# A hybrid mLSTM layer on one core: z and v projected with the tokens stationary, q moved ahead of z, PSUM banks divided three to five

## The chip, the cores and the metric

The kernel runs on 1 core of one Trainium2 chip. The metric is the device time of one execution in microseconds (us); lower is better. The kernel before takes 1349.28 us (median of 3 runs, 1349.18 to 1349.31). Engines are named as in the profile: PE (TensorE: matmuls; PEld are its weight loads), DVE (VectorE), ACT (ScalarE), POOL (GpSimd), SP (SyncE, which here issues the large loads).

## The reference

One layer on 256 prompt tokens and 64 sample tokens, width 2048, in float32:

```python
h = rmsnorm(x)
q, k, v, o, gates, u, z = split(h @ w_in)      # 512, 512, 1024, 1024, 8, 1024, 1024 columns
hm, C, n, m = mlstm_chunkwise(q, k / sqrt(128), v, ig, log_sigmoid(f), C0, n0, m0)  # 4 heads
y_m = rmsnorm_per_head(hm) * sigmoid(o)
zs = rmsnorm(gelu(z), g_sgu)                   # over the 1024 columns of z, per token
y_s = gelu(u) * (tril(w_sp) @ zs + b_sp)       # over chunks of 128 tokens
x = x + concat(y_m, y_s) @ w_out
x = x + square(relu(rmsnorm(x) @ w_ff1)) @ w_ff2
y = rmsnorm(x, g_final)
```

Outputs are y for both streams, the states C, n, m, and zs of the sample tokens. The token norm of the first line is put behind the projections: every projection is multiplied by R1, one factor per token.

## The kernel before

All 320 tokens (three blocks `TOK` of 128, 128 and 64) are worked on at once. Float32 precision is made of two reduced-precision parts: a weight tile is loaded (`raw`), ACT casts it to `hi`, DVE makes `lo = raw - hi`; activations are kept as `Xh`, `Xl` likewise. A product is hi·xh + hi·xl + lo·xh.

Most of the work stands in a list of jobs, run in order. A `Job` (L73) projects 128 output columns: the weight is stationary, 320 tokens move, 48 matmuls add up in one PSUM bank, and the result has columns on partitions and tokens along the row. `evac` then takes it out of the bank. The list begins with 8 jobs of z, 4 of q, 8 of v, 8 of o, 8 of u; then 16 of w_out and, four times, 16 of w_ff1 and 4 `Group`s of w_ff2 (L103). A `Group` has the tokens stationary instead: 512 weight columns move in 8 chunks of 2x128 rows, and the result comes out with tokens on partitions. k and the gates are projected in a loop of their own ahead of the list (`kacc`, `gacc`).

z and v are wanted with tokens on partitions (v as the moving operand of the heads, z for the spatial gating). So each of their jobs is followed by three transposes on PE into a bank (`zt`, `vt`), which DVE and ACT then read (`z_side`, `v_side`). The norm over z's columns is summed on POOL into `sacc`, and PE adds it up over the partitions (`ssz`).

Engines run their queues in the order of the code (a manual schedule). Smaller work is written as coroutines: `later(gen, d)` enters one, and `run_side`, called ahead of each job, runs the next piece of every coroutine that is due (`cur` counts the jobs). Such are the gate chain (`gates`), z's transposes, and the four heads. `head(h)` has three pieces:

- the scores S = k·q and the transposed k (`kt`) into two banks; DVE and ACT make P (`Pm`, `Ph`, `Pl`), `kh`, `kl` and others of them;
- 24 matmuls into three banks T and two more, `cs` and `cs2`; then DVE and ACT form the head's norm from T (`den`, `hsq`, `rsqrt_to`, `hmt`), and the new state `co` from `cs` and `cs2` (L611: `co` from `cs2`);
- six transposes of `hmt` (`hT`).

`v_evac` enters `head(i // 2)` after every second v job, so heads start two jobs apart. PSUM has 8 banks of 128x512 float32: 2 with the tag "mm" (`mmt`, for projections) and 6 with "sd" (`sdt`, everything else). A tile that wants a bank waits until what was in the bank has been read.

Weight halves are split (`split_until`) four ahead of the one that PE works on; ACT's and DVE's queues hold these splits between the evacuations and the pieces of the coroutines.

Of the kernel before, what the change touches and what calls it, by code (L numbers as in the profile page):

```python
# [50 lines left out]
def emit(tc, A):  # L51
# [51 lines left out]
    class Group:  # L103
# [6 lines left out]
        def __init__(self, src, q, g):  # L110
            self.src, self.q, self.g = src, q, g
            self.raw, self.hi, self.lo = ([None] * GC for _ in range(3))

        def load(self, c):
            self.raw[c] = wp.tile([P, 2, GN], F32, tag="raw", name=f"raw_g{self.q}{self.g}_{c}", bufs=4)
            sp.dma_start(self.raw[c][:], self.src[:, 2 * c:2 * c + 2, :])

        def split(self, c):
            hi = wp.tile([P, 2, GN], F32R, tag="hi", name=f"hi_g{self.q}{self.g}_{c}")
            lo = wp.tile([P, 2, GN], F32R, tag="lo", name=f"lo_g{self.q}{self.g}_{c}")  # L120
            act.copy(hi[:], self.raw[c][:])  # L121
            dve.tensor_tensor(lo[:], self.raw[c][:], hi.bitcast(F32)[:], ALU.subtract)  # L122
            self.hi[c], self.lo[c] = hi, lo

        def matmuls(self, after):

            n = f"{self.q}{self.g}"
            last = GC - 1
            back = sdt(f"gt{n}") if self.q == QUARTERS - 1 else None
            ga = [mmt(f"ga{n}_0"), mmt(f"ga{n}_1"), sdt(f"ga{n}_2")]  # L130
            gl = [sdt(f"gl{n}_{m}") for m in range(GM)]
            for c in range(GC):
                for kk in range(2):
                    k = 2 * c + kk
                    hi = self.hi[c][:, kk, :]
                    if k == 0:
                        pe.matmul(ga[2][:], hs[k][:], hi, start=True, stop=False)
                    for j in range(2):
                        t0, w = TOK[j]
                        pe.matmul(ga[j][:], hid[k][0][:, t0:t0 + w], hi, start=k == 0, stop=False)  # L140
                        pe.matmul(ga[j][:], hid[k][1][:, t0:t0 + w], hi, start=False, stop=k == KT - 1)  # L141
                    if k:
                        pe.matmul(ga[2][:], hs[k][:], hi, start=False, stop=k == KT - 1)  # L143
# [12 lines left out]
                after(c, back)  # L156
# [74 lines left out]
    for k in range(KT):  # L231
# [6 lines left out]
        act.activation(Xh[k][:], xr, AF.Copy, scale=gk)  # L238
# [8 lines left out]
        dve.scalar_tensor_tensor(Xl[k][:], xr, gk, Xh[k].bitcast(F32)[:], ALU.mult, ALU.subtract)  # L247
# [14 lines left out]
        for h in range(H):  # L262
            pe.matmul(kacc[h][:, :NT], hi[:, h * P:h * P + P], Xh[k][:], start=first, stop=False)
        for h in range(H):
            pe.matmul(kacc[h][:, :NT], hi[:, h * P:h * P + P], Xl[k][:], start=False, stop=False)
        for h in range(H):
            pe.matmul(kacc[h][:, :NT], lo[:, h * P:h * P + P], Xh[k][:], start=False, stop=last)
        pe.matmul(gacc[:100, :NT], hi[:, 4 * P:], Xh[k][:], start=first, stop=False)
        pe.matmul(gacc[:100, :NT], hi[:, 4 * P:], Xl[k][:], start=False, stop=last)
# [20 lines left out]
    zs = [None] * 4  # L290
    vT = [None] * 8
# [23 lines left out]
    rz = ap.tile([P, 3], F32, name="rz")  # L315
    Y = [None] * KT
# [31 lines left out]
    def gates():  # L348
# [5 lines left out]
        rsqrt_to(R1[:], s[:, :NT], D, tmp320, "r1")  # L354
        yield
# [83 lines left out]
    def z_evac(c):  # L439
        def evac(acc):  # L440
            t = tmp320(f"zr{c}")
            dve.tensor_tensor(t, acc, R1[:], ALU.mult)
            gz = tmp320(f"gz{c}")
            act.activation(gz, t, AF.Gelu_apprx_tanh)
            if c == 0:
                act.activation(sacc[:], gz, AF.Square)
                pool.tensor_scalar(sacc[:], sacc[:], D // 2 * EPS / P, None, ALU.add)
            else:
                act.activation(t, gz, AF.Square)
                pool.tensor_tensor(sacc[:], sacc[:], t, ALU.add)  # L450
            later(z_side(c, gz), 3 - c % 2)
        return evac

    def z_side(c, gz):
        if c == 0:
            z01 = ap.tile([P, 2, 8, P], F32, tag="big", name="z01", bufs=2)
            z2g = ap.tile([P, 2, 8, P], F32, tag="big", name="z2g", bufs=2)
            zs[:] = [z01[:, 0], z01[:, 1], z2g[:, 0], z2g[:, 1]]
            zs.append(z01)
            pool.memset(zs[2][NS:], 0.0)  # L460
            sp.dma_start(zs[3], A["gsgu"].partition_broadcast(P))
        pt = sdt(f"zt{c}")
        for j, (t0, n) in enumerate(TOK):
            pe.transpose(pt[:n, P * j:P * j + P], gz[:, t0:t0 + n], ident[:])
        dve.tensor_copy(zs[4][:, :, c, :], pt[:, 0:256].rearrange("p (j c) -> p j c", c=P))
        dve.tensor_copy(zs[2][:NS, c, :], pt[:NS, 256:384])
        if c < 7:
            return
        yield
        st = sdt("ssz")  # L470
        for j, (t0, n) in enumerate(TOK):
            pe.matmul(st[:n, 2 * j:2 * j + 2], sacc[:, t0:t0 + n], ones[:, 0:2], start=True, stop=True)
        s3 = small(P, 3)("z3s")
        pool.memset(s3, 1.0)
        for j, (t0, n) in enumerate(TOK):
            dve.tensor_copy(s3[:n, j:j + 1], st[:n, 2 * j:2 * j + 1])
# [35 lines left out]
    def v_evac(i):  # L512
        def evac(acc):
            t = tmp320(f"vT{i}")
            dve.tensor_tensor(t, acc, R1[:], ALU.mult)
            later(v_side(i, t), 2)
            if i % 2:
                later(head(i // 2), 2)
        return evac

    def v_side(i, t):
        h, e = divmod(i, 2)
        pt = sdt(f"vt{i}")
        for j, (t0, n) in enumerate(TOK):
            pe.transpose(pt[:n, P * j:P * j + P], t[:, t0:t0 + n], ident[:])
        vh, vl = vau_h[h % 2], vau_l[h % 2]
        for sl, n, c0, c1 in ((slice(0, 2), P, 0, 256), (slice(2, 3), NS, 256, 384)):
            src = pt[:n, c0:c1].rearrange("p (j c) -> p j c", c=P)
            dst = (slice(0, n), sl, slice(e * P, e * P + P))
            act.copy(vh[dst], src)  # L530
            dve.tensor_tensor(vl[dst], src, vh.bitcast(F32)[dst], ALU.subtract)
        return
        yield
# [140 lines left out]
    x2rhs = lambda k: (X2[k][0][:], X2[k][1][:])  # L674
# [24 lines left out]
    def out_evac(m):  # L699
        def evac(acc):  # L700
            dve.tensor_tensor(xres[m], acc, xres[m], ALU.add)
            h_ = xp.tile([P, NT], F32R, tag=f"xh{m}", name=f"x2h{m}")
            l_ = xp.tile([P, NT], F32R, tag=f"xl{m}", name=f"x2l{m}")
            act.activation(h_[:], xres[m], AF.Copy, scale=g2(m))
            dve.scalar_tensor_tensor(l_[:], xres[m], g2(m), h_.bitcast(F32)[:],
# [87 lines left out]
    halves = [(j, i) for j in jobs + [group] for i in range(GC if isinstance(j, Group) else 2)]  # L793
# [23 lines left out]
    for i, job in enumerate(jobs):  # L817
        cur[0] = i
# [6 lines left out]
        if i in pre:  # L825
            pre[i]()
        if isinstance(job, Group):
            def after(c, pt):
# [4 lines left out]
                if pt is not None and job.g == 0 and c == 3:  # L833
                    for i in range(8):
                        gfb.append(xp.tile([P, NT], F32, tag=f"xh{i}", name=f"gfb{i}"))
# [18 lines left out]
    ga = [mmt("ga0"), mmt("ga1"), sdt("ga2")]  # L854
# [109 lines left out]

def _arrays(i):
# [5 lines left out]
    for n, width in (("q", 512), ("k", 512), ("v", 1024), ("o", 1024), ("g", 8), ("u", 1024),  # L971
# [21 lines left out]
        "w_q": _tiles(cols["q"]), "w_v": _tiles(cols["v"]), "w_o": _tiles(cols["o"]),  # L993
        "w_u": _tiles(cols["u"]), "w_z": _tiles(cols["z"]),
# [33 lines left out]
```

## Time and profile before

| | |
|---|---|
| time, median of 3 runs | 1349.28 us |
| the profiled execution | 1349.38 us, span 1347.7 us |
| PE busy | 1337.1 us (99%) |
| DVE, ACT, POOL busy | 711.9, 563.7, 19.2 us |
| z jobs (with q) on PE | from 38.6 us |
| v jobs on PE | from 127.1 us |
| w_out jobs on PE | from 323.8 us |
| read from HBM | 202.7 MB |

A row of the timeline has its start, its length, engine, line, operation, output and inputs, and how many were merged (xN); in brackets, the idle time before it and what ended that. Matmuls overlap: their lengths add up to more than the time they take, so starts are compared.

### The profile page before, as it was taken

What the parts mean: (1) busy time and instruction counts of PE and PEld (TensorE: products, weight loads), DVE (VectorE), ACT (ScalarE), POOL (GpSimd) and SP (SyncE); (2) the same over time, 40 slices, a digit from 0 to 9 for tenths busy, and PEclk for the clock granted to TensorE, in tenths of its full rate; (3) what the DMA queues carried; (4) which work ended last, traced back from release to release, by engine and by line L of the source; (5) the groups of instructions that cost most, each with busy time, mean ns of one, the idle gap of its engine ahead of it and who ended that gap; (6) DMA issues with size and microseconds to landing.
All of it is one profiled execution on the core that took longest, in us unless ns stands there. A gap on an engine that the chain in (4) does not pass through costs nothing.

```text
span 1347.7 us, 20742 instructions
## 1 busy us (share of the span) xinstructions
PE 1337.1 (99%) x8409; PEld 1277.4 (95%) x8409; DVE 711.9 (53%) x1064; ACT 563.7 (42%) x907; POOL 19.2 (1%) x57
## 2 busy tenths in 40 slices
PE   9999999999999999999999999999999999999997
PEld 9999999999999999988999988899998889998885
DVE  8676565555555544444444454454444454444665
ACT  7544556444443444333344343234442334443333
POOL 1120000000000000000000000000000000000000
PEclk9999999999999999999999999999999999999999
DMA  8645433545444444445444355444445545445442
GB/s 277 212 147 184 130 131 113 171 140 195 166 157 154 138 147 157 157 141 159 150 145 156 126 169 163 152 141 157 152 145 159 155 127 170 149 145 185 132 141 78
DMA packets 60883, 208.01 MB, mean 154 GB/s; under 512 B 6816, under 2 KB 8736, under 8 KB 60788
## 3 DMA queue, kind: packets, MB, share of 16 engines
q1 hardware_dynamic: 57796, 200.53, 46.5%
q10 hardware_dynamic: 2960, 6.12, 1.3%
q8 instruction: 66, 1.08, 0.3%
q14 instruction: 29, 0.24, 0.1%
q0 software_dynamic: 32, 0.03, 0.0%
HBM read 202.72 MB, written 3.94 MB: 153 GB/s over the span
## 4 chain that ended last, share of the span: by engine, by line
PE 99%; DMA 0%; DVE 0%; ACT 0%; SPq 0%; issue 0%; DVEq 0%; ACTq 0%
PE acc_f L97 11%; PE acc_f L101 11%; PE acc_f L98 11%; PE gl L150 10%; PE ga L141 8%; PE ga L140 8%; PE ga L143 4%; PE acc_out L97 3%; PE acc_out L101 3%; PE acc_out L98 3%; PE acc_u L97 1%; PE acc_v L101 1%; PE acc_z L101 1%; PE acc_v L97 1%; PE acc_o L101 1%; PE acc_o L97 1%
## 5 line engine op out<-in xcount | busy, mean ns | idle before, releaser
L97 PE MATMUL acc_f<-x2h,hi_f 128*128 128x320 f32 x1024 | 302.6, 309 | 0.0
L98 PE MATMUL acc_f<-x2l,hi_f 128*128 128x320 f32 x1024 | 302.4, 309 | 0.0
L122 DVE TENSOR_TENSOR lo_g<-raw_g,hi_g 128x1024 fp32r<-128x1024 f32 x128 | 153.5, 1223 | 129.6 <-PE gl L150 88.1
L121 ACT CAST hi_g<-raw_g 128x1024 fp32r<-128x1024 f32 x128 | 132.2, 1049 | 200.4 <-PE ga L143 175.9
L97 PEld LDWEIGHTS acc_f<-x2h,hi_f 128*128 128x128 f32 x1024 | 192.3, 188 | 0.1
L98 PEld LDWEIGHTS acc_f<-x2l,hi_f 128*128 128x128 f32 x1024 | 192.2, 188 | 0.1
L140 PE MATMUL ga<-hi_g,Yh 128*128 128x512 f32 x480 | 188.7, 393 | 0.0
L141 PE MATMUL ga<-hi_g,Yl 128*128 128x512 f32 x480 | 188.4, 392 | 0.0
L87 DVE TENSOR_TENSOR lo_f<-raw_f,hi_f 128x1024 fp32r<-128x1024 f32 x128 | 151.5, 1222 | 59.4 <-ACT hi_f L86 39.3
L101 PE MATMUL acc_f<-x2h,lo_f 128*128 128x320 f32 x1024 | 171.0, 309 | 0.0
L150 PE MATMUL gl<-Yh,lo_g 128*128 128x320 f32 x960 | 159.7, 308 | 0.0
L150 PEld LDWEIGHTS gl<-Yh,lo_g 128*128 128x128 f32 x960 | 150.1, 188 | 9.5
L101 PEld LDWEIGHTS acc_f<-x2h,lo_f 128*128 128x128 f32 x1024 | 155.4, 188 | 0.0
L86 ACT CAST hi_f<-raw_f 128x1024 fp32r<-128x1024 f32 x128 | 128.8, 1046 | 37.5 <-PE ga L143 31.3
L729 ACT ACTIVATE f<-f 128x320 f32<-128x320 f32 x64 | 30.2, 472 | 254.3 <-DVE f L728 254.3
L140 PEld LDWEIGHTS ga<-hi_g,Yh 128*128 128x128 f32 x480 | 90.2, 188 | 16.4 <-DVE f L728 1.3
L141 PEld LDWEIGHTS ga<-hi_g,Yl 128*128 128x128 f32 x480 | 90.2, 188 | 16.0
L728 DVE SCALAR_TENSOR_TENSOR f<-acc_f,R 128x320 f32<-128x320 f32 x64 | 31.5, 492 | 132.5 <-PE acc_f L101 132.3
L143 PE MATMUL ga<-hi_g,hs 128*128 128x512 f32 x225 | 87.9, 391 | 0.0
L98 PE MATMUL acc_out<-Yl,hi_out 128*128 128x320 f32 x256 | 75.6, 309 | 0.0
L97 PE MATMUL acc_out<-Yh,hi_out 128*128 128x320 f32 x256 | 75.6, 309 | 0.0
L338 DVE TENSOR_TENSOR Yl<-f,Yh 128x320 fp32r<-128x320 f32 x64 | 31.5, 492 | 65.9 <-ACT Yh L337 65.9
(358 smaller groups left out, 1931.3 us busy)
## 6 DMA issues: line engine op xcount, KB each, us to landing
raw_f<-w_ff SPq DMA_DIRECT2D x128, 512.0 KB, 4.3
raw_g<-w_ff SPq DMA_DIRECT2D x128, 512.0 KB, 3.9
raw_out<-w_out SPq DMA_DIRECT2D x32, 512.0 KB, 4.6
raw_z<-w_z SPq DMA_DIRECT2D x16, 512.0 KB, 5.3
raw_v<-w_v SPq DMA_DIRECT2D x16, 512.0 KB, 5.2
raw_o<-w_o SPq DMA_DIRECT2D x16, 512.0 KB, 5.0
raw_u<-w_u SPq DMA_DIRECT2D x16, 512.0 KB, 4.6
w0raw<-w SPq DMA_DIRECT2D x15, 306.0 KB, 4.4
```

Source lines behind the costliest of these rows:

```text
L86: act.copy(hi[:], raw[:])
L87: dve.tensor_tensor(lo[:], raw[:], hi.bitcast(F32)[:], ALU.subtract)
L97: pe.matmul(o, self.hi[h][:, k, :], xh, start=(h == 0 and k == 0), stop=False)
L98: pe.matmul(o, self.hi[h][:, k, :], xl, start=False, stop=False)
L101: pe.matmul(o, self.lo[h][:, k, :], xh, start=False, stop=(h == 1 and k == 7))
L121: act.copy(hi[:], self.raw[c][:])
L122: dve.tensor_tensor(lo[:], self.raw[c][:], hi.bitcast(F32)[:], ALU.subtract)
L140: pe.matmul(ga[j][:], hid[k][0][:, t0:t0 + w], hi, start=k == 0, stop=False)
L141: pe.matmul(ga[j][:], hid[k][1][:, t0:t0 + w], hi, start=False, stop=k == KT - 1)
L143: pe.matmul(ga[2][:], hs[k][:], hi, start=False, stop=k == KT - 1)
L150: pe.matmul(gl[m][:, :NT], self.lo[c][:, kk, m * P:m * P + P], hid[k][0][:], start=k == 0, stop=k == KT - 1)
L338: dve.tensor_tensor(l_[:], src, h_.bitcast(F32)[:], ALU.subtract)
```

## The change

- z and v are no longer 16 `Job`s but 4 of a new kind, `Rows` (two groups of 512 columns each): tokens stationary, 512 weight columns moving, in 8 chunks of 16 matmuls. The three token blocks come out with tokens on partitions in three banks. For the third block, Xh and Xl of the 64 sample tokens are put side by side as one stationary operand of 128 columns (`pair`), whose two halves of the result are added.
- Xh and Xl become the halves of one tile.
- The transposes `zt` and `vt`, and the sums `ssz` on PE, are gone. R1 is also wanted by rows: it goes through DRAM (`rd`) into `rt`, with four DMAs on POOL's queue. ACT applies it while it applies gelu to z or casts v, and sums the squares of z.
- q's four jobs stand ahead of z; `q_evac` also makes the `pair` tiles, eight copies in each.
- Inside a `Rows` group, `cur` goes up ahead of chunks 2, 4 and 6, so a group has four steps of the coroutines.
- `v_evac` enters two heads at the end of a group, the first with a delay of 1 and the second of 2.
- Tag "mm" gets three banks and "sd" five; the third accumulator of a w_ff2 `Group` moves from "sd" to "mm".

```diff
-        return ps.tile([P, 512], F32, tag="mm", name=name, bufs=2)
+        return ps.tile([P, 512], F32, tag="mm", name=name, bufs=3)
...
-        return ps.tile([P, 512], F32, tag="sd", name=name, bufs=6)
+        return ps.tile([P, 512], F32, tag="sd", name=name, bufs=5)
...
+    class Rows(Chunks):
+        def __init__(self, src, name, evac):
+            super().__init__(src, name)
+            self.evac = evac
+
+        def matmuls(self, before, after):
+            acc = [mmt(f"ga_{self.name}_{j}") for j in range(3)]
+            for c in range(GC):
+                before(c)
+                for j, (t0, n) in enumerate(TOK):
+                    for k in (2 * c, 2 * c + 1):
+                        hi, lo = self.hi[c][:, k % 2, :], self.lo[c][:, k % 2, :]
+                        first, last = k == 0, k == KT - 1
+                        xh, xl = Xh[k][:, t0:t0 + n], Xl[k][:, t0:t0 + n]
+                        if j < 2:
+                            pe.matmul(acc[j][:], xh, hi, start=first, stop=False)
+                            pe.matmul(acc[j][:], xl, hi, start=False, stop=False)
+                            pe.matmul(acc[j][:], xh, lo, start=False, stop=last)
+                            continue
+                        if not first:
+                            pe.matmul(acc[j][:NS, :], xh, lo, start=False, stop=False)
+                        pe.matmul(acc[j][:], pair[k], hi, start=first, stop=last)
+                        if first:
+                            pe.matmul(acc[j][:NS, :], xh, lo, start=False, stop=False)
+                    if c == GC - 1:
+                        self.evac(j, acc[j])
+                after(c, None)
...
-            ga = [mmt(f"ga{n}_0"), mmt(f"ga{n}_1"), sdt(f"ga{n}_2")]
+            ga = [mmt(f"ga{n}_{j}") for j in range(3)]
...
+        rd = dr.tile([1, NT], F32, name="rd")
+        pool.dma_start(rd[:], R1[0:1, :])
+        for j, (t0, n) in enumerate(TOK):
+            pool.dma_start(rt[:n, j:j + 1], rd[0, t0:t0 + n].unsqueeze(1))
...
+    def z_evac(g):
+        def evac(j, acc):
...
+            z = zs[j][:n, 4 * g:4 * g + 4, :].rearrange("p a b -> p (a b)")
+            src = acc[:n, :]
+            if j == 2:
+                dve.tensor_copy(z, acc[:NS, :])
+                dve.tensor_tensor(z, acc[NS:, :], z, ALU.add)
+                src = z
+            act.activation(z, src, AF.Gelu_apprx_tanh, scale=rt[:n, j:j + 1])
+            for i in range(2):
+                t = tmp320(f"zq{g}{j}{i}")
+                act.activation(t[:n, :256], z[:, 256 * i:256 * i + 256], AF.Square,
+                               accum_out=zsq[:n, j, 2 * g + i:2 * g + i + 1])
+            if g and j == 2:
+                later(z_norm(), 1)
...
     def q_evac(h):
         def evac(acc):
             dve.tensor_tensor(qT[h][:], acc, R1[:], ALU.mult)
+            for k in range(4 * h, 4 * h + 4):
...
+                act.copy(pair[k][:, :NS], Xh[k].bitcast(F32)[:, NP:])
+                act.copy(pair[k][:, NS:], Xl[k].bitcast(F32)[:, NP:])
...
-            later(v_side(i, t), 2)
-            if i % 2:
-                later(head(i // 2), 2)
+    def v_evac(g):
+        def evac(j, acc):
+            n = TOK[j][1]
+            src = acc[:n, :]
+            if j == 2:
+                low = ap.tile([P, 512], F32, tag="gb", name=f"vs{g}", bufs=2)
+                dve.tensor_copy(low[:NS, :], acc[:NS, :])
+                dve.tensor_tensor(low[:NS, :], acc[NS:, :], low[:NS, :], ALU.add)
+                src = low[:NS, :]
+            r = rt[:n, j:j + 1]
+            for i in range(2):
+                vh, vl, x = vau_h[i], vau_l[i], src[:, DV * i:DV * i + DV]
+                act.activation(vh[:n, j, :DV], x, AF.Copy, scale=r)
+                dve.scalar_tensor_tensor(vl[:n, j, :DV], x, r, vh.bitcast(F32)[:n, j, :DV],
+                                         ALU.mult, ALU.subtract)
+            if j == 2:
+                later(head(2 * g), 1)
+                later(head(2 * g + 1), 2)
...
-    for c in range(8):
-        add(A["w_z"][c], z_evac(c), xrhs, f"z{c}")
     for h in range(H):
         add(A["w_q"][h], q_evac(h), xrhs, f"q{h}")
-    for i in range(8):
-        add(A["w_v"][i], v_evac(i), xrhs, f"v{i}")
+    for g in range(2):
+        jobs.append(Rows(A["w_z"][g], f"z{g}", z_evac(g)))
+    for g in range(2):
+        jobs.append(Rows(A["w_v"][g], f"v{g}", v_evac(g)))
...
+        if isinstance(job, Rows):
+            def before(c):
+                if c and c % 2 == 0:
+                    cur[0] += 1
+                    run_side()
+
+            def after(c, pt):
+                base[0] += 1
+                split_until(base[0] + 4)
+
+            job.matmuls(before, after)
+            continue
```

Where the heads stand moves with it. On PE before, head 1's scores and transposes stand here (S1 and kt1 are tiles of head 1, hT0 of head 0, vt3 and acc_v5 of v's jobs; the bracket names the engine whose work the instruction waits for):

```order
L618 MATMUL hT0_0_2068<-ident_144,hmt_615 128x128 [waits DVE_49,Activation_49]
L618 MATMUL hT0_0_2068<-ident_144,hmt_615 128x128 [waits Activation_49] x2
L618 MATMUL hT0_1_2074<-ident_144,hmt_615 128x128 x3
L525 MATMUL vt3_2080<-ident_144,vT3_1934 128x128 x2
L525 MATMUL vt3_2080<-ident_144,vT3_1934 64x128
L540 MATMUL S1_2088<-qT1_582,kT1_586 128x256
L541 MATMUL S1_2088<-qT1_582,kT1_586 128x128
L542 MATMUL S1_2088<-qT1_582,kT1_586 64x64
L545 MATMUL kt1_2092<-ident_144,kT1_586 128x128 [waits Activation_49]
```

On PE in the changed kernel they stand right behind the last matmuls of head 0's second piece (cs2 of head 0 is printed as cs20), ahead of chunk 2 of group v1:

```order
L611 MATMUL cs20_1774<-vauh0_581,kh_597 128x258
L612 MATMUL cs20_1774<-vaul0_583,kh_597 128x258
L613 MATMUL cs20_1774<-vauh0_581,kl_598 128x258
L577 MATMUL S1_1810<-qT1_566,kT1_570 128x256 [waits DVE_49]
L578 MATMUL S1_1810<-qT1_566,kT1_570 128x128
L579 MATMUL S1_1810<-qT1_566,kT1_570 64x64
L582 MATMUL kt1_1814<-ident_128,kT1_570 128x128 [waits Activation_49]
L582 MATMUL kt1_1814<-ident_128,kT1_570 128x128
L582 MATMUL kt1_1814<-ident_128,kT1_570 64x128
L138 MATMUL ga_v1_0_1702<-hi_v1_2_1628,x4_90 128x512
```

So S1 moved from behind hT0, with a v job between, to directly behind cs20, and it got a wait for DVE, kt1 one for ACT. Heads 2 and 3 stand to each other in the same way, behind job o0.

On DVE before, head 0's P stands behind the evacuation of one v job and the two halves of its transposed copy (`vaul0` from vt1):

```order
L87 TENSOR_TENSOR lo_v4_0_1821<-raw_v4_0_1672,hi_v4_0_1820 128x1024
L87 TENSOR_TENSOR lo_v4_1_1827<-raw_v4_1_1740,hi_v4_1_1826 128x1024
L515 TENSOR_TENSOR vT2_1830<-acc_v2_1769,R1_80 128x320
L531 TENSOR_TENSOR vaul0_599<-vt1_1832,vauh0_597 128x2x128
L531 TENSOR_TENSOR vaul0_599<-vt1_1832,vauh0_597 64x128
L548 TENSOR_TENSOR P0_1848<-S0_1840,Ea0_1538 128x256
```

On DVE in the changed kernel it stands behind the evacuation of the whole group v0 and a split:

```order
L565 SCALAR_TENSOR_TENSOR vaul0_583<-ga_v0_0_1455,rt_609,vauh0_581 128x256
L565 SCALAR_TENSOR_TENSOR vaul1_584<-ga_v0_0_1455,rt_609,vauh1_582 128x256
L565 SCALAR_TENSOR_TENSOR vaul0_583<-ga_v0_1_1456,rt_609,vauh0_581 128x256
L565 SCALAR_TENSOR_TENSOR vaul1_584<-ga_v0_1_1456,rt_609,vauh1_582 128x256
L558 COPY vs0_1656<-ga_v0_2_1457 64x512
L559 TENSOR_TENSOR vs0_1656<-ga_v0_2_1457,vs0_1656 64x512
L565 SCALAR_TENSOR_TENSOR vaul0_583<-vs0_1656,rt_609,vauh0_581 64x256
L565 SCALAR_TENSOR_TENSOR vaul1_584<-vs0_1656,rt_609,vauh1_582 64x256
L118 TENSOR_TENSOR lo_v1_3_1666<-raw_v1_3_1580,hi_v1_3_1665 128x1024
L585 TENSOR_TENSOR P0_1677<-S0_1669,Ea0_1363 128x256
```

Between P0 and the head's norm two splits `lo` stand late in both; before, one evacuation of a v job (`vT3`) follows them.

More of the change, by code (lines that the diff above doesn't have):

```diff
@@ L141, in matmuls @@
                         pe.matmul(ga[j][:], hid[k][1][:, t0:t0 + w], hi, start=False, stop=k == KT - 1)
-                    if k:
-                        pe.matmul(ga[2][:], hs[k][:], hi, start=False, stop=k == KT - 1)
+                    pe.matmul(ga[2][:], hs[k][:], hi, start=k == 0, stop=k == KT - 1)
                 if c == last:
@@ L262, in emit @@
         for h in range(H):
-            pe.matmul(kacc[h][:, :NT], hi[:, h * P:h * P + P], Xh[k][:], start=first, stop=False)
+            pe.matmul(kacc[h][:, :NT], hi[:, h * P:h * P + P], Xh[k], start=first, stop=False)
         for h in range(H):
-            pe.matmul(kacc[h][:, :NT], hi[:, h * P:h * P + P], Xl[k][:], start=False, stop=False)
+            pe.matmul(kacc[h][:, :NT], hi[:, h * P:h * P + P], Xl[k], start=False, stop=False)
         for h in range(H):
-            pe.matmul(kacc[h][:, :NT], lo[:, h * P:h * P + P], Xh[k][:], start=False, stop=last)
-        pe.matmul(gacc[:100, :NT], hi[:, 4 * P:], Xh[k][:], start=first, stop=False)
-        pe.matmul(gacc[:100, :NT], hi[:, 4 * P:], Xl[k][:], start=False, stop=last)
+            pe.matmul(kacc[h][:, :NT], lo[:, h * P:h * P + P], Xh[k], start=False, stop=last)
+        pe.matmul(gacc[:100, :NT], hi[:, 4 * P:], Xh[k], start=first, stop=False)
+        pe.matmul(gacc[:100, :NT], hi[:, 4 * P:], Xl[k], start=False, stop=last)
     C0 = ap.tile([P, H, VP], F32, name="C0")
@@ L290, in emit @@
     zs = [None] * 4
+    pair = [None] * KT
     vT = [None] * 8
@@ L436, in gates @@
             act.activation(Eb[h][:, :256], gb[:, 256:], AF.Exp, scale=-1.0)
[L439 to L451, printed above, removed]
-        return evac
@@ L454, in z_side @@
[L454 to L472, printed above, removed]
+    def z_evac(g):
+        def evac(j, acc):
+            n = TOK[j][1]
+            if zs[0] is None:
+                z01 = ap.tile([P, 2, 8, P], F32, tag="big", name="z01", bufs=2)
+                z2g = ap.tile([P, 2, 8, P], F32, tag="big", name="z2g", bufs=2)
+                zs[:] = [z01[:, 0], z01[:, 1], z2g[:, 0], z2g[:, 1]]
+                pool.memset(zs[2][NS:], 0.0)
+                sp.dma_start(zs[3], A["gsgu"].partition_broadcast(P))
+            z = zs[j][:n, 4 * g:4 * g + 4, :].rearrange("p a b -> p (a b)")
[11 more added lines that the diff above has]
+                later(z_norm(), 1)
+        return evac
@@ L473, in z_side, with z_norm @@
+    def z_norm():
         s3 = small(P, 3)("z3s")
-        pool.memset(s3, 1.0)
-        for j, (t0, n) in enumerate(TOK):
-            dve.tensor_copy(s3[:n, j:j + 1], st[:n, 2 * j:2 * j + 1])
+        pool.memset(s3, D // 2 * EPS)
+        for i in range(4):
+            for j, n in ((slice(0, 2), P), (slice(2, 3), NS)):
+                dve.tensor_tensor(s3[:n, j], s3[:n, j], zsq[:n, j, i], ALU.add)
         rsqrt_to(rz[:], s3, D // 2, small(P, 3), "rz")
@@ L509, in evac @@
             dve.tensor_tensor(qT[h][:], acc, R1[:], ALU.mult)
[L510 to L533 removed]
+            for k in range(4 * h, 4 * h + 4):
+                if k % 2 == 0:
+                    both = yslot("l", 8 + k // 2, f"pair{k}", F32R)
+                pair[k] = both[:, P * (k % 2):P * (k % 2) + P]
+                act.copy(pair[k][:, :NS], Xh[k].bitcast(F32)[:, NP:])
+                act.copy(pair[k][:, NS:], Xl[k].bitcast(F32)[:, NP:])
+        return evac
+    def v_evac(g):
+        def evac(j, acc):
+            n = TOK[j][1]
+            src = acc[:n, :]
[13 more added lines that the diff above has]
+                later(head(2 * g + 1), 2)
+        return evac
     hm = [None] * H
@@ L791, in emit @@
     group = jobs.pop()
-    halves = [(j, i) for j in jobs + [group] for i in range(GC if isinstance(j, Group) else 2)]
+    halves = [(j, i) for j in jobs + [group] for i in range(GC if isinstance(j, Chunks) else 2)]
     loaded = [0]
@@ L853, in emit @@
     gt = sdt("gt")
-    ga = [mmt("ga0"), mmt("ga1"), sdt("ga2")]
+    ga = [mmt(f"ga{j}") for j in range(3)]
     sml = [bp[0].tile([P, 5], F32, name=f"sml{j}") for j in range(3)]
```

51 lines of the change are left out of this document (29 added, 22 removed).

## The prediction

> **What bounds the kernel now.** I read the page first: its span, the share of each engine, the granted clock, and the chain that ended last.
>
> ```profile
> span 1347.7 us, 20742 instructions
> PE 1337.1 (99%) x8409; PEld 1277.4 (95%) x8409; DVE 711.9 (53%) x1064; ACT 563.7 (42%) x907; POOL 19.2 (1%) x57
> ...
> PEclk9999999999999999999999999999999999999999
> ...
> PE 99%; DMA 0%; DVE 0%; ACT 0%; SPq 0%; issue 0%; DVEq 0%; ACTq 0%
> ```
>
> TensorE (PE) is busy for 99% of the span and carries the whole chain. So the change is worth the time that it takes out of PE's stream, less what it puts in, less any time in which it makes PE wait. VectorE (DVE) and ScalarE (ACT) are half idle and matter only where PE waits for them. My sum is made against the profiled execution, 1349.38 us (the span of 1347.7 and 1.7 around it); the median of the runs, 1349.28, is 0.1 lower.
>
> **PE's stream: out and in.** The timeline gives starts, and since matmuls overlap, the distance between starts is what one costs.
>
> ```profile
> 59.94 0.82 PE L464 MATMUL zt<-ident,gz 128*128 128x128 f32 x6
> 60.52 0.39 PE L97 MATMUL acc_z<-xh,hi_z 128*128 128x320 f32 x1
> ...
> 112.22 0.81 PE L472 MATMUL ssz<-ones,sacc 128*128 128x2 f32 x6
> 112.96 0.42 PE L97 MATMUL acc_q<-xh,hi_q 128*128 128x320 f32 x1
> ...
> 127.14 0.31 PE L97 MATMUL acc_v<-xh,hi_v 128*128 128x320 f32 x1
> 134.18 0.31 PE L97 MATMUL acc_v<-xh,hi_v 128*128 128x320 f32 x1
> ...
> 141.22 0.49 PE L525 MATMUL vt<-ident,vT 128*128 128x128 f32 x3
> 141.47 0.39 PE L97 MATMUL acc_v<-xh,hi_v 128*128 128x320 f32 x1
> 141.70 0.30 PE L98 MATMUL acc_v<-xl,hi_v 128*128 128x320 f32 x1
> ...
> 1311.72 0.48 PE L867 MATMUL ga<-hi_g,Yh 128*128 128x512 f32 x1
> 1312.04 0.39 PE L869 MATMUL ga<-hi_g,Yl 128*128 128x512 f32 x1
> 1312.26 0.40 PE L871 MATMUL ga<-lo_g,Yh 128*128 128x512 f32 x1
> ...
> 1315.48 0.60 PE L775 MATMUL gt<-ident,xres 128*128 128x128 f32 x4
> ```
>
> Out: 16 jobs of z and v. One job of 48 matmuls runs from 127.14 to 134.18, 7.04 us; 16 are 112.6. The z transposes: four places of 0.58 (59.94 to 60.52), after each of which the first matmul takes 0.23 instead of 0.147 (141.47 to 141.70; 7.04/48): 2.6. The v transposes: eight of 0.25 (141.22 to 141.47), a little more where S follows, and one such return: 2.4. The sums over z (ssz): 0.74. Together 118.4.
>
> In: 4 groups of 8 chunks, each of 16 matmuls of 512 columns. The final group of w_ff2 already runs exactly this shape and order: from 1311.72 to 1315.48, 3.76 us, of which 0.09 is the first step after transposes (0.32 instead of 0.23). So 3.67 a chunk, and 32 chunks are 117.4. The ends: 0.22 a step (1312.04 to 1312.26) would give 112.6, and 3.76 in every chunk 120.3. I take 117.4, a whole chunk of the same shape. **Net -1.0 us** (ends -5.8 and +1.9). The transposes are gained, but 512 matmuls of 512 columns move 7% more columns than 768 of 320.
>
> Here a rule of the Trainium skill speaks otherwise ("TensorE: Matmul & The Clock Gate", Part 2, back-to-back issue gap): it gives a sustained 131 ns for a matmul of 512 columns with its weight load. By it the 32 chunks would take 67 us, an estimate, 50 less than my term. The rows above have 229 ns for just this pair, so I follow the rows.
>
> **What PE comes to wait for.** Head h makes seven tiles of the small PSUM pool: S, kt, three T, cs and cs2. Before, two jobs lie between the starts of two heads: S1 follows hT0, when head 0's tiles have been read. Now head 2g+1 starts one step after head 2g: PE issues T, cs, cs2 of head 0 and, with nothing between, S1 and kt1; after job o0 the same for heads 2 and 3. There are five banks, and T (3), cs and cs2 hold all five. S1 waits for DVE's reading of cs2 (`co`, the last step of head 0's norm), kt1 for ACT's `hmt` from T0; everything behind them on PE waits too. The trace of before shows how long that norm takes:
>
> ```profile
> 148.92 0.60 PE L540 MATMUL S<-qT,kT 128*128 128x256 f32 x2
> ...
> 150.23 0.39 PE L97 MATMUL acc_v<-xh,hi_v 128*128 128x320 f32 x1
> 150.48 0.41 DVE L548 TENSOR_TENSOR P<-S,Ea 128x256 f32<-128x256 f32 x1
> ...
> 155.23 2.36 DVE L87 TENSOR_TENSOR lo_v<-raw_v,hi_v 128x1024 fp32r<-128x1024 f32 x2 [0.32 <-ACT hi_v L86]
> ...
> 157.35 0.28 PE L574 MATMUL T<-vauh,Ph 128*128 128x258 f32 x1
> 157.55 0.49 DVE L515 TENSOR_TENSOR vT<-acc_v,R 128x320 f32<-128x320 f32 x1
> 157.99 0.22 DVE L598 TENSOR_SCALAR h0d<-T,emT 128x1 f32<-128x1 f32 x1
> 159.84 0.18 DVE L600 RECIPROCAL h0d<-h0d 128x3 f32<-128x3 f32 x1
> 160.25 0.49 PE L525 MATMUL vt<-ident,vT 128*128 128x128 f32 x3
> 161.91 1.28 ACT L176 ACT_TABLE_LOAD   x1
> 164.11 0.42 DVE L611 TENSOR_TENSOR co<-cs,co 128x257 f32<-128x257 f32 x1
> 164.23 1.19 ACT L609 ACTIVATE hmt<-T,h0q 128x256 f32<-128x256 f32 x3 [0.82 <-DVE h0q L607]
> ```
>
> PE is through with T, cs, cs2 at 160.25, 2.9 after it began; `co` ends at 164.53, and the first `hmt` (a third of 1.19) at 164.63. **So at the least each of the two places costs 4.3 us.** Then, DVE comes to the norm late. Before, P follows S by 1.56, the pair of lo splits ends 7.11 after P's start (157.59), and the norm begins at 157.99, 0.64 after T. Now the group's evacuation stands ahead of P:
>
> ```profile
> 145.08 1.05 ACT L86 CAST hi_v<-raw_v 128x1024 fp32r<-128x1024 f32 x1
> 149.12 0.37 ACT L530 CAST vauh<-vt 128x256 fp32r<-128x256 f32 x1 [2.99 <-PE vt L525]
> 149.53 0.43 DVE L531 TENSOR_TENSOR vaul<-vt,vauh 128x256 fp32r<-128x256 f32 x1 [0.24 <-ACT vauh L530]
> ...
> 575.82 1.37 DVE L747 COPY tsum<-ga 128x512 f32<-128x512 f32 x2 [3.79 <-PE ga L141]
> 577.46 0.39 PE L137 MATMUL ga<-hi_g,hs 128*128 128x512 f32 x1
> ```
>
> Count from PE's end of group v0. The pieces of 256 columns go back and forth between ACT and DVE (0.37, 0.43) and DVE is through with the second block's at about 1.2. The copy and the sum for the third block, 512 columns, are 0.69 each: 2.6. ACT's two casts: 3.35; hi 1.05: 4.4; lo (half of 2.36) 1.2: P starts at 5.6, the two lo of later chunks end at 12.7. PE takes S and kt (148.92 to 150.23: 1.3, and 0.1 for the return) and two chunks (7.3) and begins T at 8.7, ending at 11.6. From the norm's start DVE needs six small steps of 0.24 (1.45), and from the reciprocal to `co`'s end 4.7 (159.84 to 164.53): S1 starts at 18.85. **PE waits 7.2 us.** After v1 the same, with one job o0 (7.04) where two chunks were, so T begins at 8.4 and ends at 11.3, and with o0's evacuation (0.49, as vT) ahead of the norm: S3 starts at 19.3, **a wait of 8.0 us**. Sum 15.2; ends 4.3 twice, 8.6, and 1.5 more each, 18.2. I take 15.2, since program order puts that work ahead on DVE.
>
> **The clock** after such a wait:
>
> ```profile
> 1.12 3.78 PE L219 MATMUL warm<-ones 128*128 128x128 f32 x16 [1.12 <-DVE eps L168]
> 4.55 0.61 PE L263 MATMUL kacc<-xh,w0hi 128*128 128x320 f32 x1
> ...
> 1338.00:1340.00 2.00, 0.47 (x3) 0.03 (x1) 1.50 (x4) 0.53 (x1) 0.00 (x0) 1.00 0.63 235
> ...
> 1342.00:1344.00 2.00, 0.00 (x0) 0.00 (x0) 0.82 (x3) 0.54 (x1) 0.00 (x0) 0.82 0.35 76
> 1344.00:1346.00 2.00, 0.00 (x0) 0.00 (x0) 0.00 (x0) 0.00 (x0) 0.00 (x0) 0.50 0.92 186
> ```
>
> These columns end with granted clock, DMA share, GB/s. PE's last matmul ends at 1338.47; with a mean of 0.82 over 1342 to 1344 and 0.50 behind it, the clock fell near 1343.3, 4.8 us later. Waits of 7.2 and 8.0 are longer, so I count two falls. Coming back: 16 warm matmuls take 3.43 us (1.12 to 4.55), 0.21 each, where six fp32 transposes of the same size take 0.58 (59.94), 0.10 each; so PE ran at half speed for at least 3.4 us after its first work. Half of that is lost: 1.7 a fall; at the other end, a second such stretch, 3.4; nothing, if the clock holds. I take 2.0 each: **+4.0**.
>
> The Trainium skill ("TensorE: Matmul & The Clock Gate", Part 1, what's actually happening) has the clock halved after an idle window of about 3.4 us that runs free of the kernel. By it a wait of 7 us always holds such a window, and one of 4.3 in about a quarter of cases (an estimate, (4.3 - 3.4)/3.4). No trace here has a wait between those.
>
> **Costed at nothing.** (a) The 32 pair copies of 128x64 stand on ACT in the four q jobs:
>
> ```profile
> L568 ACT CAST qp<-qi 128x64 fp32r<-128x64 f32 x4 | 1.0, 243 | 0.0
> ```
>
> 32 of 0.243 is 7.8, and eight hi of 1.05 are 8.4, in the 28 us of four jobs; the splits run four halves (14 us) ahead. Without that cover PE would wait at most their 7.8. (b) q's move, with its four gate steps: same jobs, same steps in between, same 32 loads of z and v at 512 KB on SP. Only g_sgu's load moves behind z's first group; its reader comes a group later. (c) Four DMAs for R1 by rows on POOL's queue, which is busy 19 us in all; behind them stand the gate chain's memsets, steps later. They are read 60 us later; if late, group z0's banks are held and PE waits once. (d) z's evacuation: banks are reclaimed one block after the other, 1.4 us apart, as they are evacuated. (e) w_ff2's third accumulator shares the pool of three: two reads of 0.69 end at 577.19, and PE wants that bank at 577.46 plus four steps of 0.23, 578.4; 1.2 to spare.
>
> **Sum:** 1349.4 - 1.0 + 15.2 + 4.0 = **1367.6 us**, slower by 1.35%. Its own range is 1362 to 1372.
>
> **Rivals.** (1) *Not slower: the bank is free.* If the count that S1 waits for were reached before PE gets there (11.6 on the clock above), by DVE's reading of S0 and kt0 (through before the pair of lo, 155.23 - 150.48 after P's start, so at 10.3), PE would never stop: 1349.4 - 1.0 = 1348.4, within 0.2% (2.7 us, about what these runs can tell from no change). For it: the order names only the engine waited for. Against: S1 is issued behind cs2, and five tiles in five banks leave none. 6%. (2) *DVE is not late and the clock holds*: the norm begins 0.64 after T as now, 4.3 twice: 1357.0; with the clock lost, 1361. For it: DVE is 53% busy. Against: the splits stand ahead in program order. 18%. (3) *More waits*: each of the four ends of a group also holds PE, by the 1.4 us of the copy and sum or by ACT's squares: up to 1.5 each, 1373.6. Against: three banks come free in the order they are wanted. 10%. (4) *The step does not grow with the columns*: 512 columns at the 0.147 of 320 would be 75.3 for the four groups, 42 less: 1325. Against: the chunk from 1311.72, at 0.229 a step. 1%. The Trainium skill's 131 ns, on the page named above, is of this kind.
>
> The forecast itself has 65%. The range 1356 to 1373 holds it, rival 2, and what of rival 3 is smallest. Faster by over 0.2%: 2%; within 0.2%: 6%; slower: 92%.
>
> **What would show it.** PE's idle time before S (heads 1 and 3) near 7 and 8 us, released by DVE's `co` or ACT's `hmt`, and none elsewhere; a granted clock near half for some 3 to 4 us behind each; no zt, vt or ssz; a chunk of z or v in 3.67 us. The forecast is wrong if S1 starts within 1 us of cs2's end, if DVE begins the norm right behind T, if the clock stays at 1.00 through a 7 us wait, or if PE waits at a group's end.

## The result, and the profile after

The changed kernel takes 1367.18 us (median of 4 runs, 1366.49 to 1367.59), the kernel before 1349.3 beside it: 1.0131 times as long, 95% interval 1.0114 to 1.0149. The forecast was 1367.6.

The page after: the span, the busy time of the engines, and PE's busy time and granted clock in 40 slices of 34 us.

```profile
span 1364.8 us, 20132 instructions
...
PE 1340.1 (98%) x8099; PEld 1254.7 (92%) x8099; DVE 706.2 (52%) x1041; ACT 576.8 (42%) x952; POOL 12.0 (1%) x53
...
PE   9999897999999999999999999999999999999997
...
PEclk9999988999999999999999999999999999999999
```

PE has 310 matmuls fewer than before, but its busy time is 3 us longer. In two slices, 136 to 171 and 205 to 239 us, it is no longer full, and the clock is lower from 171 to 239. The waits of PE say what it waited for (total, times, longest, in us):

```profile
PE S L577 <- DVE co L648: 13.9, 2, 7.1
...
PE T L612 <- DVE Cl L604: 0.2, 1, 0.2
```

13.9 us in two waits, both of S for DVE's `co`; in the kernel before, the same view has only 1.1 and 0.2 us, both ahead of the first job. The timeline of PE at the first place and around it, with the starts of z and v, and of w_out at the end:

```profile
66.96 0.39 PE L138 MATMUL ga_z<-hi_z,x 128*128 128x512 f32 x1
...
70.62 0.39 PE L138 MATMUL ga_z<-hi_z,x 128*128 128x512 f32 x1
...
110.86 0.35 PE L465 MATMUL gmT_ps<-ident,GM 36*128 36x36 f32 x3
111.14 0.49 PE L138 MATMUL ga_z<-hi_z,x 128*128 128x512 f32 x1
...
125.87 0.39 PE L138 MATMUL ga_v<-hi_v,x 128*128 128x512 f32 x1
...
155.06 0.59 PE L577 MATMUL S<-qT,kT 128*128 128x256 f32 x2
...
163.81 0.28 PE L611 MATMUL T<-vauh,Ph 128*128 128x258 f32 x1
...
166.90 0.28 PE L613 MATMUL cs<-vauh,kl 128*128 128x258 f32 x1
173.93 1.22 PE L577 MATMUL S<-qT,kT 128*128 128x256 f32 x2 [6.75 <-DVE co L648]
...
178.32 0.63 PE L139 MATMUL ga_v<-hi_v,x 128*128 128x512 f32 x1
178.75 0.57 PE L140 MATMUL ga_v<-lo_v,x 128*128 128x512 f32 x1
179.15 0.39 PE L138 MATMUL ga_v<-hi_v,x 128*128 128x512 f32 x1
179.38 0.39 PE L139 MATMUL ga_v<-hi_v,x 128*128 128x512 f32 x1
...
223.25 1.22 PE L577 MATMUL S<-qT,kT 128*128 128x256 f32 x2 [7.15 <-DVE co L648]
...
341.49 0.31 PE L97 MATMUL acc_out<-Yh,hi_out 128*128 128x320 f32 x1
```

S1 stands idle 7 us behind the last cs2 (166.90). The steps of 512 columns behind it take 0.43 (178.32 to 178.75) and then, from 179.15, 0.23 again. The clock in stretches of 2 us around that place (the columns end with clock, DMA share, GB/s; PE's busy time comes first):

```profile
166.00:168.00 2.00, 1.17 (x10) 0.97 (x8) 2.00 (x3) 0.58 (x1) 0.00 (x0) 1.00 0.17 16
...
172.00:174.00 2.00, 0.07 (x1) 0.08 (x1) 0.98 (x5) 1.17 (x4) 0.14 (x2) 0.57 0.06 25
174.00:176.00 2.00, 2.00 (x7) 1.48 (x8) 0.00 (x0) 1.02 (x4) 0.00 (x0) 0.50 0.04 13
...
178.00:180.00 2.00, 2.00 (x8) 1.61 (x7) 1.13 (x5) 1.38 (x5) 0.00 (x0) 0.72 0.00 0
180.00:182.00 2.00, 2.00 (x11) 1.51 (x10) 1.68 (x3) 1.09 (x2) 0.32 (x1) 1.00 0.01 4
```

A mean of 0.57 over two us means that the clock fell near 172.3, 5.1 after PE stopped at 167.2; it was back near 179.1, 5.2 after PE went on. This takes it that the clock is either full or half, as in the undivided rows (1.00 and 0.50). DVE shows why `co` came when it did:

```profile
160.90 0.42 DVE L585 TENSOR_TENSOR P<-S,Ea 128x256 f32<-128x256 f32 x1
...
165.67 2.36 DVE L118 TENSOR_TENSOR lo_v<-raw_v,hi_v 128x1024 fp32r<-128x1024 f32 x2 [0.32 <-ACT hi_v L117]
167.94 0.21 DVE L635 TENSOR_SCALAR h0d<-T,emT 128x1 f32<-128x1 f32 x1
...
173.45 0.42 DVE L648 TENSOR_TENSOR co<-cs,co 128x257 f32<-128x257 f32 x1
```

P starts 5.84 after the end of group v0 (155.06), where the prediction had 5.6; the pair of lo ends at 12.97 (12.7); the norm begins only then, 4.1 after T's first matmul (163.81), where the kernel before has 0.64; S1 starts at 18.87 (18.85), 0.06 after `co` ends.

Worked out from starts on PE, the 17.1 us of the span are: the two places where cs and cs2 should take 1.09 and take 8.01 and 8.38 with the wait, +14.2 (6.9 and 7.3; the brackets' 6.75 and 7.15 count only from the end of the last matmul); slow steps behind them, +2.5 and +1.7; T0 and T2, which take 2.11 and 2.44 instead of 1.79, +1.0; all else up to the start of w_out -1.7 (17.7 in all there, 341.49 against 323.8); and -0.6 behind it.

### The profile page after: what moved, and what is told of

Its sections match the earlier page's. It is cut to its first block, busy times and chain, and to the rows that moved or that the text cites. A ratio compares the mean times of both kernels' runs of the same rounds, so it can differ in the third digit from the quotient of the medians.

```text
span 1364.8 us, 20132 instructions
## 1 busy us (share of the span) xinstructions
PE 1340.1 (98%) x8099; PEld 1254.7 (92%) x8099; DVE 706.2 (52%) x1041; ACT 576.8 (42%) x952; POOL 12.0 (1%) x53
## 4 chain that ended last, share of the span: by engine, by line
PE 95%; DVE 2%; ACT 1%; issue 1%; DMA 0%; SPq 0%; DVEq 0%; ACTq 0%
PE acc_f L98 11%; PE acc_f L101 11%; PE acc_f L97 11%; PE gl L184 10%; PE ga L176 8%; PE ga L175 8%; PE ga L177 4%; PE acc_out L98 3%; PE acc_out L101 3%; PE acc_out L97 3%; PE acc_u L97 1%; PE acc_u L101 1%; PE acc_u L98 1%; PE acc_o L97 1%; PE acc_o L98 1%; PE acc_o L101 1%
## 5 line engine op out<-in xcount | busy, mean ns | idle before, releaser
L97 PE MATMUL acc_f<-x,hi_f 128*128 128x320 f32 x1024 | 302.6, 309 | 0.0
L98 PE MATMUL acc_f<-x,hi_f 128*128 128x320 f32 x1024 | 302.4, 309 | 0.0
L98 PEld LDWEIGHTS acc_f<-x,hi_f 128*128 128x128 f32 x1024 | 192.2, 188 | 0.1
L97 PEld LDWEIGHTS acc_f<-x,hi_f 128*128 128x128 f32 x1024 | 192.2, 188 | 0.1
L101 PE MATMUL acc_f<-x,lo_f 128*128 128x320 f32 x1024 | 171.0, 309 | 0.0
L101 PEld LDWEIGHTS acc_f<-x,lo_f 128*128 128x128 f32 x1024 | 155.5, 188 | 0.0
L177 PE MATMUL ga<-hi_g,hs 128*128 128x512 f32 x240 | 93.8, 391 | 0.0
```

Of the source, the lines that this page charges most:

```text
L97: pe.matmul(o, self.hi[h][:, k, :], xh, start=(h == 0 and k == 0), stop=False)
L98: pe.matmul(o, self.hi[h][:, k, :], xl, start=False, stop=False)
L101: pe.matmul(o, self.lo[h][:, k, :], xh, start=False, stop=(h == 1 and k == 7))
L177: pe.matmul(ga[2][:], hs[k][:], hi, start=k == 0, stop=k == KT - 1)
```

## The experiments

The theory after the result: PE stops at S1 and S3 because the five banks of "sd" are held by the other head, the wait is as long as DVE's norm of that head, which comes late, and the clock falls for it. Rivals: that DVE and ACT can't do the heads' work in the time that is left, wherever S1 stands; that the groups of 512 columns cost more than the jobs did; that the slow steps have another cause than the idle time.

**e1: heads two steps apart.**

```diff
-                later(head(2 * g + 1), 2)
+                later(head(2 * g + 1), 3)
```

> One number undone: head 2g+1 enters two steps after head 2g instead of one, so that S1 stands behind hT0 and S3 behind hT2, with two chunks or one job between. Theory (PE stops at S1 and S3 because T, cs and cs2 of the other head hold all five banks, and then runs at half clock): both waits and both falls of the clock go. Changed kernel 1367.2, less waits of 6.9 and 7.3, less 2.5 and 1.7 for the clock: 1348.8, with PE waiting only some tenths at T0 and T2. Rival (DVE and ACT can't do a head's work in the time that is left, wherever S1 stands): the wait moves to T1 or hT1, 1357 or more. Rival (the time is lost in the groups of 512 columns): no change, 1367.

1350.67 us (11 runs), 1.0009 times the time before (1.0001 to 1.0018). One changed delay takes back 16.5 of the 17.9 us, so the groups themselves cost nothing that can be seen here, and the waits at S are gone. The longest waits of PE that remain behind the start:

```profile
PE T L611 <- ACT qp L605: 0.9, 1, 0.9
PE hT L655 <- ACT hmt L646: 0.3, 1, 0.3
...
```

It is 1.9 over the 1348.8 expected. Starts on PE show where: T2 takes 3.64 instead of 1.79, hT2 1.21, hT0 0.97 instead of 0.57. With heads further apart, ACT and DVE are still at head 1's norm when group v1 ends, so v1's evacuation, and P2 behind it, come later (7.05 after S2, against 5.84 in the changed kernel). A small part of the first rival was true.

**e2: both heads of a pair one step later, still one step apart.**

```diff
-                later(head(2 * g), 1)
-                later(head(2 * g + 1), 2)
+                later(head(2 * g), 2)
+                later(head(2 * g + 1), 3)
```

> Both heads of a pair enter one step later, still one step apart. S1 stands right behind cs2 as in the changed kernel, but the group's evacuation is through before P0, so DVE should reach the head's norm as soon as T is done. Theory (two parts of the wait: 4.3 us that the norm takes at the least, and the rest because DVE comes late): waits of 4.3 to 4.7 instead of 6.9 and 7.3, and 1.0 less at T0 and T2: 1360.8 if the clock still falls twice, 1356.6 if it never does. Rival (the wait is as long as the heads' small steps alone take, and lateness plays no part): waits stay near 7, 1366 to 1367.

1361.39 us (4 runs), ratio 1.0090 (1.0076 to 1.0104), against 1360.8 expected with both falls of the clock. PE's waits for `co`, PE's timeline at S1, and DVE's:

```profile
PE S L577 <- DVE co L648: 8.4, 2, 4.2
```

```profile
171.68 0.28 PE L611 MATMUL T<-vauh,Ph 128*128 128x258 f32 x1
...
178.91 1.22 PE L577 MATMUL S<-qT,kT 128*128 128x256 f32 x2 [4.19 <-DVE co L648]
...
172.30 0.22 DVE L635 TENSOR_SCALAR h0d<-T,emT 128x1 f32<-128x1 f32 x1 [1.13 <-PE T L613]
```

DVE now waits for T and begins the norm 0.62 after T starts; each wait is 4.2, the least that the prediction worked out (4.3). So of the changed kernel's waits (6.75 and 7.15 counted in the same way), 4.2 is the norm itself and the rest is DVE's lateness. The clock fell both times even so; around the first wait:

```profile
176.00:178.00 2.00, 0.00 (x0) 0.00 (x0) 0.36 (x3) 1.71 (x4) 0.00 (x0) 0.92 0.01 4
178.00:180.00 2.00, 1.09 (x3) 0.91 (x4) 0.79 (x4) 1.45 (x4) 0.14 (x2) 0.50 0.00 0
```

**e3: S3 and kt3 in banks of the other pool.** No instruction moves.

```diff
-        s = sdt(f"S{h}")
+        bank = mmt if h == 3 else sdt
+        s = bank(f"S{h}")
...
-        pk = sdt(f"kt{h}")
+        pk = bank(f"kt{h}")
```

> Only S3 and kt3 take their banks from the pool of three that the projections use (two are idle among the o jobs); every instruction stays where it is in each engine's row. Theory (S3 waits for a bank and nothing else): the second wait goes, and with it its fall of the clock, 7.3 + 1.7; the first stays at 6.9: 1358.2. PE goes on to job o1 while DVE does the norm of head 2. Rival (PE would wait there in any case, for DVE's or ACT's results of head 2, or for the evacuation of o0): the wait moves behind kt3 to o1, 1366 to 1367.

1357.96 us (4 runs), ratio 1.0065 (1.0049 to 1.0080). PE's timeline at the second place, and its waits:

```profile
215.40 0.28 PE L614 MATMUL cs<-vauh,kl 128*128 128x258 f32 x1
215.52 0.59 PE L578 MATMUL S<-qT,kT 128*128 128x256 f32 x2
...
217.00 0.41 PE L97 MATMUL acc_o<-x,hi_o 128*128 128x320 f32 x1
```

```profile
PE S L578 <- DVE co L649: 6.7, 1, 6.7
```

S3 starts 0.12 after the last cs2, and job o1 runs on while DVE does head 2's norm. The first wait, left as it was, is unchanged (6.7). The bank was what S3 waited for.

**e4: work for PE in the two waits.** The extra matmuls add zeros to an accumulator of v1, or write a bank that nobody reads.

```diff
+    def fill(h):
+        if h == 1:
+            for _ in range(44):
+                pe.matmul(rows[0][:NS, :NT], zero[:], Xh[0], start=False, stop=False)
+        else:
+            b = mmt("fill")
+            for _ in range(46):
+                pe.matmul(b[:, :NT], Xh[1][:, :P], Xh[0], start=True, stop=True)
...
+        if h % 2:
+            fill(h)
         s = sdt(f"S{h}")
```

> Extra matmuls that change nothing stand ahead of S1 (44 of 320 columns, with a stationary operand of zeros) and of S3 (46, into a bank that nobody reads), 6.5 and 6.8 us of work in the two waits; all else as in the changed kernel. Theory (4.2 of the loss is PE's clock, which falls because PE stands idle): the granted clock stays at 1.00, S1 and S3 begin when they did, and what follows runs at full speed: 1363.0. Rival (the slow matmuls behind the waits are not due to the idle time): 1367.2, or more if the extra matmuls come in the way.

1362.40 us (4 runs), ratio 1.0096 (1.0083 to 1.0110). PE's timeline behind the first wait, and the clock there:

```profile
174.16 0.70 PE L593 MATMUL S<-qT,kT 128*128 128x256 f32 x2 [0.39 <-DVE co L664]
...
176.12 0.40 PE L141 MATMUL ga_v<-lo_v,x 128*128 128x512 f32 x1
176.36 0.40 PE L139 MATMUL ga_v<-hi_v,x 128*128 128x512 f32 x1
```

```profile
172.00:174.00 2.00, 1.77 (x13) 1.35 (x11) 0.88 (x5) 1.17 (x3) 0.11 (x2) 1.00 0.07 27
174.00:176.00 2.00, 1.84 (x11) 1.56 (x12) 0.73 (x4) 1.26 (x4) 0.03 (x1) 1.00 0.00 0
```

S1 starts when it did, 8.0 after the first `cs`; the steps behind it take 0.24, and the clock stays at 1.00. From S1 to hT0 it is 8.85 us instead of 11.18, from S3 to hT2 8.54 instead of 10.17: 4.0 in the profiled executions, 4.8 between the medians. The slow steps were due to the idle time, and that was worth 4.

**e5, e6, e7: all heads two steps apart and one step later.** In these three, head 1's T stands behind v1's evacuation in program order, so head 1 reads the v that belongs to head 3; their times are read for the waits only.

```diff
-                later(head(2 * g), 1)
-                later(head(2 * g + 1), 2)
+                later(head(2 * g), 2)
+                later(head(2 * g + 1), 4)
```

> Heads two steps apart as in the first experiment (1350.7), and all four one step later, delays of 2 and 4. The first experiment left small waits of PE: T0 and T2 took 0.3 and 1.85 more than 1.79, the hT 0.4 and 0.6 more. Theory (these come from the evacuation of the whole group standing ahead of P0 and P2 on DVE and ACT): one step later P follows S at once, T0 and T2 take 1.8 again: 1348.5, below the kernel before. Rival (the heads' small steps are too tight against the splits with the groups of 512 columns, wherever they stand): the waits move to T1, T3 or the hT and the time stays at 1350 to 1351.

1352.30 us (11 runs), ratio 1.0022 (1.0013 to 1.0031); 3.8 over what was expected, since I had not seen that dependence. PE's first wait, and the clock behind it:

```profile
PE T L611 <- ACT vauh L564: 2.3, 1, 2.3
```

```profile
196.00:198.00 2.00, 2.00 (x13) 2.00 (x12) 1.88 (x5) 0.00 (x0) 0.00 (x0) 0.60 0.00 0
```

T0, T2 and T3 take 1.8 as foreseen, but T1 takes 5.38: it waits for the evacuation of v1. The clock falls for this wait too, near 196.4, when PE is already at work again; half speed until near 199.8 (0.54 over 198 to 200) costs about 1.7, an estimate, half of those 3.4 us. From S2 on nothing waits.

> As e5_later_apart, and the five small steps on the old state and on q (co from C0, Ch, Cl and the two of qp) stand ahead of P, in time in which DVE and ACT wait for S. If T still waits for these steps, as T2 did for qp in the first experiment, some tenths less than e5_later_apart; if T waits for nothing there, or for P's own splits, the same within 0.3.

1352.81 us (7 runs), ratio 1.0025 (1.0014 to 1.0036): 0.5 more than e5, intervals overlapping. T waited for other things, so the order of these steps shows no effect clear of the spread.

e7 is about the 0.6 us behind the start of w_out:

```diff
-            ga = [mmt(f"ga{n}_{j}") for j in range(3)]
+            third = mmt if self.q == QUARTERS - 1 else sdt
+            ga = [mmt(f"ga{n}_0"), mmt(f"ga{n}_1"), third(f"ga{n}_2")]
```

> As e5_later_apart, but the third accumulator of a w_ff2 group comes from the pool sd again, in the first three quarters (in the last there are not enough banks). The changed kernel's first ten matmuls of a quarter take 2.30 where those of before took 2.46, four times. If that is the accumulator's pool, three of the four starts take 2.46 again and the fourth 2.30, 0.5 us in all; if it has another cause, all four stay at 2.30.

1352.87 us (one run). The first steps of a quarter of w_ff2, in the kernel before and in e7:

```profile
550.08 0.39 PE L141 MATMUL ga<-hi_g,Yl 128*128 128x512 f32 x1
550.36 0.19 PEld L140 LDWEIGHTS ga<-hi_g,Yh 128*128 128x128 f32 x1 [0.32 <-DVE f L728]
550.36 0.50 PE L140 MATMUL ga<-hi_g,Yh 128*128 128x512 f32 x1
550.70 0.40 PE L141 MATMUL ga<-hi_g,Yl 128*128 128x512 f32 x1
```

```profile
553.93 0.40 PE L177 MATMUL ga<-hi_g,Yl 128*128 128x512 f32 x1
554.17 0.39 PE L176 MATMUL ga<-hi_g,Yh 128*128 128x512 f32 x1
```

Before, two steps take 0.28 and 0.34 where 0.23 is usual; in e7 none does, in all four quarters. So it is not the third accumulator's pool. The bracket of the row at 550.36 names what it was: the first matmul for the second accumulator waits for DVE's reading of the last w_ff1 job (`f`, L728), that is, for its bank, since "mm" had only two. With three banks no `ga` matmul there has such a wait. The new order of these matmuls (the third accumulator's first one stood first, now it stands last) was not tried alone.

**e8: the first pair as in e1, the second as in e5.** Every head reads its own v.

```diff
-                later(head(2 * g), 1)
-                later(head(2 * g + 1), 2)
+                later(head(2 * g), 1 + g)
+                later(head(2 * g + 1), 3 + g)
```

> Heads two steps apart; heads 0 and 1 with delays 1 and 3 as in the first experiment, heads 2 and 3 with 2 and 4, as in e5_later_apart. There the second pair cost PE nothing: from S2 to w_out 120.79 us, against 130.66 with one job more (7.11) in the first experiment, so 2.76 less than its 1350.7: 1347.9, some 0.1% below the kernel before. Rival (what PE waits for is set by DVE's and ACT's work as a whole and only changes place): 1350 to 1351.

1349.39 us (11 runs), ratio 0.9999 (0.9990 to 1.0008), 1.5 over the expectation: half of the gain came back as a wait of the first o job, which now follows hT1 directly:

```profile
194.36 0.82 PE L655 MATMUL hT<-ident,hmt 128*128 128x128 f32 x6
196.33 0.38 PE L97 MATMUL acc_o<-x,hi_o 128*128 128x320 f32 x1 [1.15 <-DVE vaul L565]
```

**e9: another bank for that job.**

```diff
-            acc = mmt(f"acc_{self.name}")
+            acc = (sdt if self.name == "o0" else mmt)(f"acc_{self.name}")
```

> As e8_mixed (1349.4), and job o0 takes its bank from sd, where head 1's T2 has been read when o0 begins, instead of the bank of v1's first accumulator, for whose evacuation PE waited there (1.2 us after hT1; ACT and DVE were still at head 1's norm when v1 ended). Theory (PE waited for that bank alone): 1.3 less, 1348.1, 0.1% below the kernel before. Rival (DVE and ACT are behind and the wait appears at T2 or at the next bank): 1349.4 again.

1347.81 us (11 runs), ratio 0.9988 (0.9979 to 0.9997): the wait is gone, and this version is faster than both kernels: by 0.12% than the one before, which its interval just tells from no change. Its waits of PE by the profile are one, at the very start:

```profile
PE warm L254 <- DVE eps L202: 1.1, 1, 1.1
```

## Why the prediction was right

**The stream, -1.0.** A chunk was costed at 3.67. In z it takes 3.66 (66.96 to 70.62), and the 16 chunks between 66.96 and 125.87, less 0.28 for the transposes of the gates, take 3.66 each: 58.63. The stream as a whole came out a little better, -1.7 up to w_out; where the 0.7 lies was not traced. Rival 4, a step that doesn't grow with the columns, is refuted by the same rows: the step of 512 columns was 0.229. The Trainium skill's 131 ns ("TensorE: Matmul & The Clock Gate", Part 2, back-to-back issue gap) is not what this kernel shows.

**The waits, +15.2.** Measured 14.2 (6.9 and 7.3 against 7.2 and 8.0). The working was right in each of its stations, P, lo, norm, `co`, to 0.3 us. The wait is 0.3 and 0.7 shorter because T itself began to wait: DVE's `Cl` and ACT's `qp` stand behind the late P, and T0 and T2 took 1.0 more together. The prediction had ended its working of T at PE's side and left this out. e2 and e3 show the two halves of the mechanism apart: the bank makes S wait, and DVE's lateness sets how long beyond 4.2.

**The clock, +4.0.** Measured 4.2 by the steps, 4.0 by e4: the two falls and their cause are as worked out. The size is partly luck. The prediction knew 1.7 and 3.4 a fall from its rows and took 2.0 without a row for it; half speed lasted 5.2 and 3.7 us after PE went on, and the two falls cost 2.5 and 1.7. Nor do the records show the half speed at the start of the kernel before: they grant 1.00 there, and only PE's pace speaks for it (behind the warm matmuls, four matmuls of `kacc` take 0.98 us and the next four 0.58).

**Costed at nothing.** Of (a) to (d) no wait shows: the view of PE's waits has nothing there. Item (e), the third accumulator, was looked at only for a loss; the four starts of w_ff2 gained 0.16 each, 0.6 in all, by the third "mm" bank, as the row at 550.36 under e7 reads.

**The rivals.** (1), the bank is free, is refuted by the row of S1; e3 shows what it would have been at one place. (2), DVE is not late and the clock holds, is refuted by DVE's rows; e2 made the first half of it true and gives 1361.4, just what was worked out for it with the clock lost (1361). (3), waits at the four ends of the groups, didn't come in the changed kernel, but in e8 one such wait of 1.2 did, at the end of v1.

So the sum was only 0.4 off, and luckily so, because -0.7 and -0.6 in the stream, -1.0 in the waits, +0.2 in the clock and +1.0 at T nearly cancel (-1.1 on the span, 17.1 against 18.2; the rest is the difference between the profiled execution and the median).

## What to carry to other kernels

When work moves, count the buffers that are alive at once in the new order: two coroutines one step apart here wanted seven banks of five, though DVE and ACT were about half idle. Price such a wait by following the releasing engine's queue from the last known point, with all that now stands ahead of it; its average load (52% here) did not tell how late it came. Then look at the distance in both directions: heads two steps apart freed the banks but met the next evacuation, and only other delays for the second pair and another bank for one job gave the 0.12%, about what the stream alone had promised.

## What the runs showed of the hardware

A wait of 4.2 us was enough for TensorE's clock to fall, both times in e2, and in e5 one of 2.3; the waits of 0.9 in e1 and 1.2 in e8 left it at 1.00. The time from PE's stop to the fall was 5.1 in the changed kernel's first wait and 3.0 in e2's first (0.92 over 176 to 178: near 177.7, PE's last work ending near 174.7). The clock in the changed kernel's second wait:

```profile
220.00:222.00 2.00, 0.00 (x0) 0.00 (x0) 0.17 (x1) 1.97 (x4) 0.00 (x0) 0.52 0.18 72
...
226.00:228.00 2.00, 2.00 (x13) 2.00 (x13) 1.11 (x5) 1.29 (x4) 0.00 (x0) 0.77 0.00 0
```

Worked out as above, the clock fell at 172.28 and 220.08 and came back at 179.12 and 226.92: distances of 6.84, 40.96 and 6.84, which are 2, 12 and 2 times 3.41 to within 0.04. In e2 it fell at 177.68 and 225.48 and came back at 184.52 and 228.88: 6.84, 40.96 and 3.40 apart. So in these two profiles every change lies on a grid of 3.41 us that does not follow PE's stops and starts, and what a wait cost hung on where it lay on that grid.

The Trainium skill ("TensorE: Matmul & The Clock Gate", Part 1, what's actually happening) has the clock fall after at least one idle window of about 3.4 us that runs free of the kernel. The grid agrees with windows that run free. That a whole window must be idle does not: the 3.0 is shorter than one, and in e5 the wait of 2.3 was too. So the prediction's estimate, that only about one wait of 4.3 in four would make the clock fall, is not borne out: both of e2's did. How much of a window must be idle was not measured.
